# One core, two transformer blocks: the feed-forward's two products of a weight tile in one instruction, and five smaller edits

## The chip, the core and the metric

The kernel runs on one core of a Trainium2 chip. The metric is the device time of one execution in microseconds (us); the kernel before takes 3591.42, the median of three runs (3586.63 to 3591.92). Engines: TensorE (PE, its weight loads PEld), VectorE (DVE), ScalarE (ACT), GpSimd (POOL), SyncE (SP, which issues every DMA here).

## The reference, cut to what matters

256 rows of width 2048, fp32, pass two blocks. Only the widths and the operations around the change stand here.

```python
def first_block(x, c, ...):
    mod = silu(c) @ w_ada + b_ada                       # 2048 x 12288, six parts
    shift1, scale1, gate1, shift2, scale2, gate2 = split(mod, 6)
    p = modulate(rms_norm(x, norm1_w), shift1, scale1) @ w_in   # u 1024, q 512, k 512, v 1024, o 1024, gates 16
    y_f = fourier_mix(u)                                # 2D DFT in 4 groups of 256
    y_m = mlstm_bidirectional(q, k, v, gates) * sigmoid(o)      # 4 heads, normalised rows
    x = x + gate1 * (concat([y_f, y_m]) @ w_out)
    h2 = modulate(rms_norm(x, norm2_w), shift2, scale2)
    a, v = split(depthwise_conv_centred(h2 @ w_up, w_conv, b_conv), 2)   # 2048 x 11264
    x = x + gate2 * ((silu(a) * v) @ w_down)            # 5632 x 2048
    return rms_norm(x, norm_f_w)

def second_block(x, ...):
    h = x + 0.5 * rms(swiglu(rms(x, pre1), w_gate, w_up, w_down), post1)  # 2 x 2048 x 5632, 5632 x 2048
    ...                                  # S5 state space model, sparse attention, gates, out
    return h + 0.5 * rms(swiglu(rms(h, pre2), ...), post2)               # the same widths again
```

## The kernel before

**Number format.** Every large product keeps nearly fp32 accuracy by a split into two parts, hi (`float32r`, ScalarE's copy) and lo (VectorE's difference x - hi). W·x becomes hi·xh + lo·xh + hi·xl, three TensorE products that add up in one PSUM region. Activations lie transposed: 128 features on the partitions, the 256 rows of x along the free axis, so an output tile is 128 x 256 and half of a PSUM bank.

**Weights.** A stream (`STREAMS`) is packed on the host in the order of use, in groups of output tiles; `lin_steps` (L304) goes through the groups, and through a group in chunks of 128 x 1024 weights. `chunk` (L298) loads a chunk of 512 KB by SP into `wr` (4 buffers; in the first mixer every third goes to `wa`, 2 more), ScalarE writes `wh` (3), VectorE `wl` (2). For each k of the chunk the three products run, each over the group's tiles in turn:

```python
for ci, (a, b) in enumerate(((hi, xh), (lo, xh), (hi, xl))):
    for j in js:
        self.mm(outs[j][0:widths[j]], a[:, c:c + widths[j]], b, ...)
```

A group of four tiles takes two banks of the eight. In a stream with `tile_evac` the last group takes a bank for each tile, holds back its last two chunks and ends tile by tile. `matmul` is always called in `mm` (L291), so every matmul has that line; tiles tell them apart.

**Feed-forward.** Three of them: up1/down1 (with convolution), up2/down2, up3/down3. `up` has 44 + 44 output tiles, 22 groups of two a tiles and two v tiles (`_pairs`), 16 k; `down` has 16 output tiles in groups of four, 44 k. `ev_up` (L592, L1157) takes a group's two banks: convolution or scaling, Silu, the product of both halves, and `hidden` (L628) splits it into `hh` and `hl`. `ev_down` (L613, L1171) scales a tile and adds its square; `post_norm` (L1182) then makes the next stage's input, tile by tile, and its split parts. `modulated` (L505) does that ahead of up1.

**Order around it.** `entry` (L638) sums the first two modulation parts (64 chunks of `w_ada1`) on TensorE: `strip_sum` (L470) multiplies by a single column, in four 32-column strips of the array side by side. Between them run the steps of q and k's stream (`next(stream)` twice per outer step). `mix1` (L723) then runs the streams v_in, u_in, o_in, each of 16 chunks; after each chunk `background` steps the generators in `self.bg`: the mLSTM (`mlstm`, L823), the DFT, and `rest` (L555), the modulation parts 2, 4, 3, 1.6 steps a chunk and 1.0 in out1. Part 2 is summed on VectorE (`ada_part`, L446: 32 scaled sums of 128 x 1024), parts 4 and 3 on TensorE (`ada_strips`, L475). `ev_o` forces the rest of the mLSTM at o_in's first group. In `mlstm` a row of a 36 x 256 table is spread over 128 partitions by a matmul with a column of the unit matrix, three times: in `weights` (L889), `values` (L926), and at the end for the norm.

In up2 `s5_tables` (L1001) computes 32 tables (cosine and sine, 128 x 512) in the background and stores them in DRAM; in the second mixer `load_tab` (L1387) loads each and ScalarE appends the negated sine. The order of instructions on each engine is the framework's, from its own schedule, except in two stretches that are written out by hand (`manual_schedule` in `post_norm`).

## Time and profile before

| | |
|---|---|
| runs | 3591.42 us median, 3586.63 to 3591.92 |
| profiled execution | 3595.09 us, span 3593.4 us, mean granted TensorE clock 0.988 |
| TensorE busy | 3508.3 us (98%), 28264 matmuls |
| weight loads busy | 3349.0 us (93%) |
| VectorE busy | 2198.6 us (61%) |
| ScalarE busy | 1594.4 us (44%) |
| POOL busy | 23.8 us (1%) |
| DMA | 710.8 MB, mean 198 GB/s |

"Busy" is the time in which an engine ran at least one instruction; matmuls overlap one another in the records, so the spacing of their starts tells what one costs, not its duration. "Granted clock" is the share of TensorE's 2.4 GHz that it was given (0.5 is its 1.2 GHz level). The streams run in this order (first load issued, us): entry 0, v_in 135, u_in 206, o_in 284, out1 385, up1 489, down1 1014; the second block's feed-forward from about 1280, its mixer from 2054, the last feed-forward from 2801.

### The profile page before, as it was taken

The page shows a single profiled execution, that of the slowest core. Times are in us where ns is not written, and L with a number is a line of the kernel's source. Part 1 is how long each engine was busy: PE and PEld are TensorE (multiplying, and loading weights), DVE is VectorE, ACT ScalarE, POOL GpSimd, SP SyncE. Part 2 cuts the span into 40 slices and gives each one's busy share as a digit, 9 for nine tenths or more (in the row PEclk, how much of TensorE's full clock was granted, in tenths as well). Part 3 has the DMA queues.
Part 4 walks back from the last instruction along what each step waited for, and adds up shares of the span by engine and source line. Part 5 has one row for each costly group of instructions (what it writes and reads, how often), then busy time and mean ns, then how long its engine had stood idle before and what let it go on. Part 6 is the DMA issues. An engine that isn't in the chain of part 4 may idle for free.

```text
span 3593.4 us, 67935 instructions
## 1 busy us (share of the span) xinstructions
PE 3508.3 (98%) x28264; PEld 3349.0 (93%) x28264; DVE 2198.6 (61%) x3146; ACT 1594.4 (44%) x2096; POOL 23.8 (1%) x65
## 2 busy tenths in 40 slices
PE   8999999999999999999999999899999999999997
PEld 4688889999999999999999899789899999999997
DVE  2574467777655479865544589986556655555445
ACT  2343345555444444444433443358744544444333
POOL 0000000000000000000000000000000000000000
PEclk9999999999999999999999999999999999999999
DMA  9886756777555556765555556555455455555554
GB/s 332 308 294 219 271 198 222 230 224 224 182 182 183 184 182 212 225 211 183 182 183 183 173 167 197 160 170 152 139 182 182 153 182 183 183 186 183 182 183 140
DMA packets 213318, 710.83 MB, mean 198 GB/s; under 512 B 23904, under 2 KB 39296, under 8 KB 213008
## 3 DMA queue, kind: packets, MB, share of 16 engines
q1 hardware_dynamic: 213008, 706.48, 61.4%
q8 instruction: 221, 3.62, 0.4%
q14 instruction: 89, 0.73, 0.1%
HBM read 694.29 MB, written 11.57 MB: 196 GB/s over the span
## 4 chain that ended last, share of the span: by engine, by line
PE 92%; DVE 4%; DMA 2%; issue 1%; ACT 1%; SPq 0%; DVEq 0%; ACTq 0%
PE ps L291 92%; DMA wr<-in_w_ada 1%; DVE wl L276 1%; DVE w L276 1%; DVE t L276 1%; DVE r L279 0%; DMA r<-in_xT 0%; PE ps L1637 0%; DVE r L276 0%; DVE w L1416 0%; DMA tab<-d_tab 0%; ACT wh L273 0%; DMA wr<-in_w_qk_in 0%; DMA wa<-in_w_out 0%; DVE rstd L417 0%
## 5 line engine op out<-in xcount | busy, mean ns | idle before, releaser
L276 DVE TENSOR_TENSOR wl<-wr,wh 128x1024 fp32r<-128x1024 f32 x1064 | 1300.6, 1223 | 1106.2 <-PE ps L291 869.1
L273 ACT ACTIVATE wh<-wr 128x1024 fp32r<-128x1024 f32 x1064 | 1126.6, 1059 | 1549.1 <-PE ps L291 1398.3
L291 PE MATMUL ps<-r,wh 128*128 128x256 f32 x12224 | 1762.1, 285 | 26.6 <-ACT r L273 19.1
L291 PEld LDWEIGHTS ps<-r,wh 128*128 128x128 f32 x12224 | 1596.9, 193 | 67.2 <-issue 24.7
L291 PE MATMUL ps<-r,wl 128*128 128x256 f32 x6112 | 1001.6, 286 | 14.9 <-DVE wl L276 14.8
L291 PEld LDWEIGHTS ps<-r,wl 128*128 128x128 f32 x6112 | 850.2, 193 | 35.3 <-DVE wl L276 21.6
L291 PE MATMUL ps<-hh,wl 128*128 128x256 f32 x2112 | 345.0, 283 | 0.0
L291 PE MATMUL ps<-hl,wh 128*128 128x256 f32 x2112 | 345.0, 283 | 0.0
L291 PE MATMUL ps<-hh,wh 128*128 128x256 f32 x2112 | 343.9, 283 | 0.0
L291 PEld LDWEIGHTS ps<-hl,wh 128*128 128x128 f32 x2112 | 294.0, 192 | 0.0
L291 PEld LDWEIGHTS ps<-hh,wl 128*128 128x128 f32 x2112 | 294.0, 192 | 0.0
L291 PEld LDWEIGHTS ps<-hh,wh 128*128 128x128 f32 x2112 | 293.4, 192 | 0.0
L291 PE MATMUL ps<-m,wh 128*128 128x256 f32 x1024 | 154.1, 286 | 0.4 <-ACT wh L273 0.4
L291 PEld LDWEIGHTS ps<-m,wh 128*128 128x128 f32 x1024 | 134.6, 191 | 8.0 <-issue 4.6
L291 PE MATMUL ps<-wr,silu_c 128*32 128x512 f32 x348 | 80.5, 630 | 11.8 <-DMA wr<-in_w_ada 11.7
L279 DVE SCALAR_TENSOR_TENSOR acc<-wr,silu_c,acc 128x1024 f32<-128x1024 f32 x50 | 64.1, 1282 | 35.6 <-DMA wr<-in_w_ada 35.2
L291 PE MATMUL ps<-m,wl 128*128 128x256 f32 x512 | 83.2, 284 | 0.0
L279 DVE SCALAR_TENSOR_TENSOR t<-ps,params,t 128x255 f32<-128x255 f32 x176 | 76.6, 476 | 0.6
L276 DVE TENSOR_TENSOR wl<-wa,wh 128x1024 fp32r<-128x1024 f32 (+1 forms) x34 | 40.8, 1199 | 58.1 <-ACT wh L273 29.1
L291 PEld LDWEIGHTS ps<-m,wl 128*128 128x128 f32 x512 | 70.6, 191 | 3.7 <-DVE wl L276 2.0
L273 ACT ACTIVATE t<-ps 128x256 f32<-128x256 f32 (+2 forms) x87 | 39.3, 458 | 76.0 <-PE ps L291 56.1
L273 ACT ACTIVATE t<-ps,params 128x256 f32<-128x256 f32 x88 | 46.6, 562 | 55.8 <-PE ps L291 34.8
(233 smaller groups left out, 1776.8 us busy)
## 6 DMA issues: line engine op xcount, KB each, us to landing
wr<-in_w_up SPq DMA_DIRECT2D x528, 512.0 KB, 3.7
wr<-in_w_down SPq DMA_DIRECT2D x264, 512.0 KB, 3.6
wr<-in_w_ada SPq DMA_DIRECT2D x141, 512.0 KB, 5.1
wr<-in_w_out SPq DMA_DIRECT2D x53, 512.0 KB, 3.9
wa<-in_w_ada SPq DMA_DIRECT2D x51, 512.0 KB, 5.3
wr<-in_w_ga_in SPq DMA_DIRECT2D x32, 512.0 KB, 3.7
wr<-in_w_glu SPq DMA_DIRECT2D x32, 512.0 KB, 3.7
wr<-in_w_gb_in SPq DMA_DIRECT2D x32, 512.0 KB, 3.6
```

Of the source, the lines that this page charges most:

```text
L273: return self.nc.scalar.activation(out=out, in_=in_, func=func, **kw)
L276: return self.nc.vector.tensor_tensor(out, a, b, op=op)
L279: return self.nc.vector.scalar_tensor_tensor(out=out, in0=a, scalar=s, in1=b, op0=op0, op1=op1)
L291: self.nc.tensor.matmul(out, lhsT, rhs, start=start, stop=stop, skip_group_check=skip)
```

## The change

1. The feed-forward streams run "wide": an activation's xh and xl lie side by side in one 128 x 2 x 256 tile (`pair`, in the ring of now 25 pairs; `hidden` likewise). hi multiplies both at once (512 columns, a whole bank), lo multiplies xh alone into the bank's first half, right behind. An output tile now takes a bank; groups are of two tiles. `fold` adds the two halves of the bank. `ev_up` collects two groups before Silu and product; the post-norm gain moves from `ev_down` to `post_norm`.
2. `v_in` is split; its first half (8 chunks) runs in the entry, one step per outer step, the other half (`vb_in`) in `mix1`. The sums' bank also takes the place of the separate `mods` bank.
3. In `mlstm` the rows go to DRAM (`rows_out`) and come back over 128 partitions (`row_in`), both issued by POOL.
4. While a pool with room is open (`more_lo`), every third low part lies in an extra buffer `wx`.
5. `rest` sums part 2 in strips and parts 4 and 3 on VectorE.
6. The tables are stored with three parts; the negation moves from `load_tab` to `s5_tables`, which runs at 0.34 steps a chunk where it ran at 0.45.

```diff
-    "v_in": ("w_in", 16, _tiles(_cols(O_V, 1024))),
+    "v_in": ("w_in", 16, _tiles(_cols(O_V, 512))),
+    "vb_in": ("w_in", 16, _tiles(_cols(O_V + 512, 512))),
...
-    "up1": ("w_up", 16, _pairs(KF, DFF)),
-    "down1": ("w_down", 44, _tiles(_cols(0, D))),
+    "up1": ("w_up", 16, _singles(KF, DFF)),
+    "down1": ("w_down", 44, _tiles(_cols(0, D), per=2)),
...
+    def fold(self, dst, bank):
+        self.act(dst, bank[:, 1], ACT.Copy)
+        self.tt(dst, bank[:, 0], dst, ALU.add)
+        return dst
...
-        lo = self.new(self.p_w, "wl", [P, CH], F32R, self.NB[2])
+        self.nlo += 1
+        if self.more_lo is not None and self.nlo % 3 == 0:
+            lo = self.new(self.more_lo, "wx", [P, CH], F32R, 1)
+        else:
+            lo = self.new(self.p_w, "wl", [P, CH], F32R, self.NB[2])
...
-            if spread:
+            if wide:
+                outs = banks = [self.ps() for _ in tiles]
+            elif spread:
...
+                        x = act(k)
+                        if wide:
+                            for j in js:
+                                c = (k - k0) * n + starts[j]
+                                self.mm(outs[j], hi[:, c:c + P], x, k == 0, k == kt - 1, True)
+                                self.mm(outs[j][:, 0], lo[:, c:c + P], x[:, 0], False, k == kt - 1, True)
+                            continue
...
             def rest():
-                yield from self.ada_part(2, self.mod[:, 2])
+                yield from self.ada_strips(2, self.mod[:, 2])
                 for part in (4, 3):
-                    yield from self.ada_strips(part, self.mod[:, part])
+                    yield from self.ada_part(part, self.mod[:, part])
...
             def ev_up(gi, banks):
+                if gi % 2 == 0:
+                    self.av = self.t2(), self.t2()
+                for n in range(2):
+                    t = self.fold(self.t1(), banks[n])
+                    conv(self.av[n][:, gi % 2], t, gi + n * KF)
+                if gi % 2 == 1:
+                    a, v = self.av
+                    self.act(a, a, ACT.Silu)
+                    hid.append(self.hidden(ph, a, v))
...
-                self.stt(xs[k], res, self.mod[:, 5, k:k + 1], xs[k], ALU.mult, ALU.add)
+                for part in (1, 0):
+                    self.stt(xs[k], res[:, part], self.mod[:, 5, k:k + 1], xs[k], ALU.mult, ALU.add)
...
                 if qt in (1, 4):
-                    next(stream)
+                    next(streams[0])
+                if qt == 6:
+                    next(streams[1])
...
         def weights(hd, d):
             r = d * 32 + hd
-            mb = self.ps()[:, 0]
-            self.mm(mb, self.eye[0:R, r:r + 1].to_broadcast([R, P]), mrow, True, True)
+            mb = self.row_in(0, r)
...
+    def rows_out(self, n, rows, n_rows=36):
+        self.nc.gpsimd.dma_start(self.d_rows[n, 0:n_rows], rows[0:n_rows])
+
+    def row_in(self, n, r):
+        t = self.t1()
+        d = self.d_rows[n, r]
+        self.nc.gpsimd.dma_start(t, bass.AP(tensor=d.tensor, offset=d.offset, ap=[[0, P], [1, T]]))
+        return t
...
+            self.act(tab[:, 2], tab[:, 1], ACT.Copy, scale=-1.0)
+            nc.sync.dma_start(self.d_tab[j], tab[:, 0:3])
...
-                self.ts(f, res, gp[:, k:k + 1], None, ALU.mult)
-                self.add_square(st, res)
+                f = self.fold(fhalf(), res)
+                self.add_square(st, f)
...
+                self.stt(t, fs[k], gp[:, k:k + 1], r, ALU.mult, ALU.mult)
...
-            nc.sync.dma_start(tab[:, 0:2], self.d_tab[j])
-            self.act(tab[:, 2], tab[:, 1], ACT.Copy, scale=-1.0)
+            nc.sync.dma_start(tab, self.d_tab[j])
```

## Rows read from the trace of the kernel before

**Rows 1.** The page's chain that ended last, shares by engine.

```profile
PE 92%; DVE 4%; DMA 2%; issue 1%; ACT 1%; SPq 0%; DVEq 0%; ACTq 0%
```

**Rows 2.** Stretches: us; busy of PE, PEld, DVE, ACT, POOL; clock; DMA share; GB/s.

```profile
0.00:137.00 137.00, 115.28 (x666) 62.50 (x666) 39.00 (x83) 36.96 (x59) 1.78 (x21) 0.96 0.92 332
137.00:512.00 375.00, 367.03 (x2760) 312.92 (x2760) 201.40 (x260) 145.15 (x231) 5.67 (x16) 0.98 0.74 256
...
2240.00:2410.00 170.00, 152.68 (x1157) 137.47 (x1156) 160.68 (x262) 73.94 (x108) 7.40 (x8) 0.92 0.55 168
...
2800.00:2830.00 30.00, 23.74 (x165) 22.34 (x165) 28.10 (x62) 17.61 (x36) 0.00 (x0) 0.89 0.32 100
2830.00:3300.00 470.00, 470.00 (x3911) 469.74 (x3910) 251.97 (x251) 201.41 (x210) 0.00 (x0) 1.00 0.59 183
```

**Rows 3.** TensorE's timeline in down3: start us, us to the end, what.

```profile
3553.38 0.64 PE L291 MATMUL ps<-hh,wl 128*128 128x256 f32 x4
3553.86 0.64 PE L291 MATMUL ps<-hl,wh 128*128 128x256 f32 x4
```

**Rows 4.** TensorE's timeline at up1's start, granted clock 0.5.

```profile
513.38 1.05 PE L291 MATMUL ps<-r,wl 128*128 128x256 f32 x4
514.23 2.04 PE L291 MATMUL ps<-r,wh 128*128 128x256 f32 x8
```

**Rows 5.** The timeline of gn_in2, whose weights have 48 columns.

```profile
2254.26 0.28 PE L291 MATMUL ps<-r,wl 128*48 128x256 f32 x1
...
2258.69 0.28 PE L291 MATMUL ps<-r,wl 128*48 128x256 f32 x1
```

**Rows 6.** The timeline at down3's end.

```profile
3572.82 0.28 PE L291 MATMUL ps<-hh,wl 128*128 128x256 f32 x1
3572.94 0.28 PE L291 MATMUL ps<-hl,wh 128*128 128x256 f32 x1
...
3573.50 0.59 PE L291 MATMUL ps<-acc,ones_d 128*128 128x256 f32 x2
3573.93 1.46 PE L291 MATMUL ps<-t,ones_d 128*128 128x256 f32 x6
```

**Rows 7.** Groups over the whole span, shapes apart: busy us, mean ns | idle.

```profile
L276 DVE TENSOR_TENSOR wl<-wr,wh 128x1024 fp32r<-128x1024 f32 x1063 | 1299.6, 1223 | 1105.7 <-PE ps L291 869.1 <-issue 103.6 <-ACT wh L273 83.5
...
L279 DVE SCALAR_TENSOR_TENSOR t<-ps,params,t 128x255 f32<-128x255 f32 x176 | 76.6, 476 | 0.6
...
L276 DVE TENSOR_TENSOR t<-hh,hh 128x256 f32<-128x256 f32 x128 | 46.7, 420 | 0.1
...
L273 ACT ACTIVATE t<-ps 128x256 f32<-128x256 f32 x53 | 20.1, 379 | 29.5 <-DVE r L283 15.2 <-PE ps L291 9.8 <-DVE m L283 4.5
...
L276 DVE TENSOR_TENSOR t<-r,rstd 128x256 f32<-128x256 f32 x32 | 12.0, 417 | 0.1
```

**Rows 8.** Groups from 137 to 512 us.

```profile
L279 DVE SCALAR_TENSOR_TENSOR acc<-wr,silu_c,acc 128x1024 f32<-128x1024 f32 x20 | 25.6, 1278 | 2.0 <-DMA wr<-in_w_ada 1.9
...
L291 PE MATMUL ps<-rd,eye 36*128 36x256 f32 x16 | 5.6, 428 | 0.0
L291 PE MATMUL ps<-rm,eye 36*128 36x256 f32 x16 | 5.6, 428 | 0.0
...
L291 PE MATMUL ps<-row,eye 4*128 4x256 f32 x8 | 2.4, 422 | 0.0
```

**Rows 9.** DMA issues: KB each, us to landing.

```profile
w<-d_rel SPq DMA_DIRECT2D x16, 128.0 KB, 4.5
...
d_rel<-t SPq DMA_DIRECT2D x1, 32.0 KB, 4.0
```

**Rows 10.** TensorE's timeline around a set of strip sums in out1.

```profile
393.31 1.05 PE L291 MATMUL ps<-wr,silu_c 128*32 128x512 f32 x4
394.29 0.75 PE L291 MATMUL ps<-m,wl 128*128 128x256 f32 x4
```

**Rows 11.** The negation of a table's sine, whole span.

```profile
L273 ACT ACTIVATE tab<-tab 128x256 f32<-128x256 f32 x32 | 13.3, 415 | 51.3 <-DMA tab<-d_tab 33.3 <-DVE w L276 11.6 <-DVE w L1416 3.9
```

More of the change, by code (lines that the diff above doesn't have):

```diff
@@ L64, in _pairs, with _singles @@
     return out
+def _singles(n_tiles, second):
+    return [[_cols(i * P, P), second + _cols(i * P, P)] for i in range(n_tiles)]
 Q_COLS = np.concatenate([np.concatenate([W2_Q + h * 64 + np.arange(64) for h in pr]) for pr in PAIRS])
@@ L89 @@
     "out2": ("w_out_2", 16, _tiles(_cols(0, D))),
-    "up3": (("ffn2_w_gate_2", "ffn2_w_up_2"), 16, _pairs(KF, DFF)),
-    "down3": ("ffn2_w_down_2", 44, _tiles(_cols(0, D))),
+    "up3": (("ffn2_w_gate_2", "ffn2_w_up_2"), 16, _singles(KF, DFF)),
+    "down3": ("ffn2_w_down_2", 44, _tiles(_cols(0, D), per=2)),
 }
@@ L237, in __init__ @@
         self.more = None
+        self.nlo = 0
+        self.more_lo = None
     def name(self, tag):
@@ L246, in new, with pair, halves, take @@
         return pool.tile(list(shape), dtype, tag=tag, name=self.name(tag), **kw)
-    def ring(self, dtype=F32):
-        return self.new(self.p_ring, "r", [P, T], dtype)
+    def pair(self):
+        return self.new(self.p_ring, "r", [P, 2, T], F32R)
+    def halves(self, pool, tag, bufs=None):
+        left = []
+        def take():
+            if not left:
+                t = self.new(pool, tag, [P, 2, T], F32, bufs)
+                left.extend([t[:, 1], t[:, 0]])
+            return left.pop()
+        return take
     def t1(self, dtype=F32):
@@ L309, in chunk, with lin_steps @@
         return hi, lo
-    def lin_steps(self, stream, act, evac=None, tile_evac=None):
+    def lin_steps(self, stream, act, evac=None, tile_evac=None, wide=False):
         _, kt, groups = STREAMS[stream]
@@ L574, in block1 @@
             self.finish()
-            self.more = None
+            self.more = self.more_lo = None
             del ys
@@ L592, in ev_up @@
             def ev_up(gi, banks):
-                a = self.t2()
-                v = self.t2()
-                for j in range(2):
-                    conv(a[:, j], banks[0][:, j], gi * 2 + j)
-                for j in range(2):
-                    conv(v[:, j], banks[1][:, j], KF + gi * 2 + j)
-                s = self.t2()
-                self.act(s, a, ACT.Silu)
-                hid.append(self.hidden(ph, s, v))
-            self.linear("up1", lambda k: h[k], ev_up)
+                if gi % 2 == 0:
[7 more added lines that the diff above has]
+                    hid.append(self.hidden(ph, a, v))
+            self.linear("up1", lambda k: h[k], ev_up, wide=True)
             self.finish()
@@ L811, in ev_o @@
                 for i in range(2):
-                    hi, lo = self.ring(F32R), self.ring(F32R)
-                    self.split(o[:, i], hi, lo)
-                    yo.append((hi, lo))
+                    x = self.pair()
+                    self.split(o[:, i], x[:, 0], x[:, 1])
+                    yo.append(x)
         self.linear("o_in", act_h, ev_o)
@@ L923, in inverse @@
             nc.vector.reciprocal(rd, dn)
-            held["rd"] = rd
+            self.rows_out(1 + held["pair"], rd)
         def values(hd, d):
@@ L955, in mlstm @@
             a, b = 2 * pair, 2 * pair + 1
+            held["pair"] = pair
             products(a)
@@ L1005, in slot @@
             if not halves:
-                t = self.new(pool, "hh", [P, 2, T])
-                halves.extend([t[:, 0], t[:, 1]])
+                t = self.new(pool, "hh", [P, 4, T])
+                halves.extend(t[:, i] for i in range(4))
             return halves.pop()
@@ L1153, in ffn @@
             hid = []
+            self.more_lo = ph
             if extra is not None:
-                self.bg.append([extra(ph), 0, 0.45])
+                self.bg.append([extra(ph), 0, 0.34])
             def ev_up(gi, banks):
-                g, s, u = self.t2(), self.t2(), self.t2()
-                rb = rstd().unsqueeze(1).to_broadcast([P, 2, T])
-                self.tt(g, banks[0], rb, ALU.mult)
-                self.act(s, g, ACT.Silu)
-                self.tt(u, banks[1], rb, ALU.mult)
-                hid.append(self.hidden(ph, s, u))
-            self.linear(up, lambda k: act[k], ev_up)
+                if gi % 2 == 0:
+                    self.gu = self.t2(), self.t2()
+                for n in range(2):
+                    self.fold(self.gu[n][:, gi % 2], banks[n])
+                if gi % 2 == 1:
+                    g, u = self.gu
+                    rb = rstd().unsqueeze(1).to_broadcast([P, 2, T])
+                    self.tt(g, g, rb, ALU.mult)
+                    self.act(g, g, ACT.Silu)
+                    self.tt(u, u, rb, ALU.mult)
+                    hid.append(self.hidden(ph, g, u))
+            self.linear(up, lambda k: act[k], ev_up, wide=True)
             self.finish()
@@ L1349, in ev_o @@
                     self.tt(b, b, ya[k], ALU.add)
-                    hi, lo = self.ring(F32R), self.ring(F32R)
-                    self.split(b, hi, lo)
-                    mixed.append((hi, lo))
+                    x = self.pair()
+                    self.split(b, x[:, 0], x[:, 1])
+                    mixed.append(x)
             self.linear("o2", lambda k: onsa[k], ev_o)
```

126 lines of the change are left out of this document (68 added, 58 removed).

## The prediction, made before the change was run

> **What bounds the kernel now.** I read the chain of waits first: 92% of it is TensorE at the matmul helper [rows 1]. The table of stretches, read next, says where that holds without exception: in the three feed-forward stretches TensorE is busy 470.0 of 470.0 us and its weight loader 469.7, at full granted clock, while VectorE is busy 251.97 [rows 2]. The other two blocks have the same spacing. A faster VectorE or DMA buys nothing there; fewer or shorter products do. Elsewhere it differs: the first 137 us move 332 GB/s with TensorE busy 115, so DMA bounds them; 137 to 512 us is TensorE's again with 8 us idle; 2240 to 2410 us is VectorE's (160.7 of 170), as is the start of the last feed-forward (28.1 of 30).
>
> The third view is TensorE's timeline in a down stage: four products start at 3553.38 and the next four at 3553.86, so one 128x128 by 256-column product costs 120 ns [rows 3]. One "triple" (hi·xh, lo·xh, hi·xl for one output tile and one k) is 360 ns. Count: up has 88 tiles x 16 k, down 16 x 44, together 2112 triples a feed-forward and 6336 in all: 2281 us of the 3593, spread over three blocks.
>
> **The change part by part. 1: wide products.** hi·xh and hi·xl become one 512-column product into a whole bank, lo·xh stays at 256 columns: two weight loads instead of three, the same 768 columns. So the gain is whatever of the 120 ns is not streaming. Where the granted clock is 0.5 (the 1.2 GHz level) four products of the same kind take 0.85 us, 213 ns each, which is 256 columns at one per cycle and nothing on top [rows 4]; at 2.4 GHz the columns alone would be half of it, 106.7, so 13.3 ns of the 120 are something else. Two rows say what. With 48 weight columns instead of 128 the spacing falls: 39 products between 2254.26 and 2258.69, 113.6 each [rows 5]. So some 6.5 ns hang on the weight load and 6.8 on the product itself. And a plain fp32 product with 128x128 weights holds the array 0.43 us for two, 215 ns, with its load entirely hidden [rows 6]. No row has a 512-column product of this type, so its cost is bounded: 213.3 + 2 = 215 by the fp32 row, which is as long; 213.3 + 6.8 = 220 if the product's own part stays and the load hides behind the longer stream; 226.7 if all 13.3 stay; 240 at worst, if the extra time grows with the columns. I take 220, since it alone uses rows of this very product type and needs only that 213 ns hide a load which 120 nearly hide. The triple is then 220 + 120 = 340, and 20 ns x 6336 = **127 us** gained (ends: 360 - 335 = 25 ns, 158 us; and nothing).
>
> The Trainium skill (TensorE: Matmul & The Clock Gate, Back-to-back issue gap) gives the gap of a single product as columns over 2.4 GHz plus a fixed 2.5 ns. That would be 109.2 for 256 columns, which the measured 120 refutes here; by it alone the triple would go from 327.5 to 325 and the gain, 2.5 ns x 6336, would be 16 us.
>
> That lo·xh follows hi at once into the same bank costs nothing by the trace: the last held products of the last down stage run one tile at a time, so back to back into one half bank, and still start 0.12 us apart (3572.82, 3572.94) [rows 6].
>
> The price of it: every tile needs a fold, 0.38 us on ScalarE and 0.42 on VectorE [rows 7], and groups of two tiles end twice as often. A chunk of 1024 weight columns lasts 8 triples, 2.72 us. VectorE needs in up1 per chunk 1.22 for the low part, 0.48 for the convolution (four of 0.48 a group of four chunks), 0.17 for the hidden split, a quarter of 1.28 for the modulation sums [rows 7, 8], and the folds' 0.21: 2.4 of 2.72. In up2 the tables take 0.34 steps of six products (0.42 each [rows 7], an estimated 0.35 apart) a chunk, 0.7, and the total is about 2.5. Tight, but under. The third low-part buffer lets it run 2 chunks (5.4 us) ahead, so I put the steady stretches at nothing; if that cover fails, the rival below prices it.
>
> Starts get worse, for TensorE now eats the first group in 16 x 0.68 = 10.9 us where it took 23, while its inputs come no faster. In up3 VectorE makes an input with two products and one scaled sum (0.42, 0.42, 0.48 [rows 7], an estimated 1.1 us together as ends overlap) and a low part of 1.22 per four: 22 us, 11 us of waiting where some 6 were lost before (23.7 busy of 30 [rows 2]): **+5**. In up1 two scaled sums a k make an estimated 17, 6 us of waiting against some 3 lost to the half clock there [rows 4]: **+4**. Up2's inputs come out of the down stage tile by tile, now two at the end instead of four: 0. Post-norm takes the gain along (0.48 in place of 0.42, 16 times [rows 7]) and the last tile is folded before its square (0.8): **+2** at mix2's start, **+2** at the end.
>
> **2: entry and first mixer.** Half of v is 8 chunks x 24 products x 0.12 = 23 us of TensorE, taken out of the stretch it bounds. In the entry its 4.2 MB cost 12.6 us at 332 GB/s, and say 1.4 for its last products: **-23 + 14**. The entry's idle time on TensorE holds the 23 us. Row broadcasts: three groups of matmuls, 5.6 + 5.6 + 2.4 us busy, of which I count 12 because ends overlap [rows 8]: **-12**. In their place POOL issues 4 writes and 20 reads. The before trace has no POOL transfer; the nearest are SP's small d_rel ones, 4.0 out and 4.5 us back [rows 9]. Read first by ScalarE's Relu and by VectorE's scaling: behind those two wait conversions of weights, and behind these TensorE, with two chunks in hand (5.8 us). The rows of a pair leave two steps before they are read, so 8.5 us of transfers meet some three chunks of 2.88, 8.6. I take 0; if all 24 stood bare it would be some 100 us, but none is issued right at its use. On POOL itself only the triangular selects queue behind them. Which modulation part is strip-summed: TensorE's set of strips costs 0.98 us until the next product [rows 10], 16 sets a part and an estimated tenth more for switching between product types, so one part less is **-17**; VectorE gets 32 x 1.28 = 41 us more in 137 to 512, where it is busy 201 of 375 [rows 2, 8]: about 233 of 320 after, still under. The steps come out at 64 + 32 of 99, so three are left at the end of out1, where two 1.28 us sums stand before up1's gain: **+3**. Sum of this part: -35.
>
> **3: tables in DRAM.** The negation (32 x 0.415 us on ScalarE, each behind a tab load [rows 11]) leaves the VectorE-bound stretch; ScalarE's conversions no longer stand behind it. Ends 0 and 13 us; I take **-3**. Stored in up2, ScalarE has room.
>
> Sum: -127 + 13 - 35 - 3 = **-152 us**. The profiled execution took 3595.1 (span 3593.4), 3.7 above the median of 3591.4, so I forecast 3443 for such a run and 3440 as the median.
>
> **The rivals.** (a) All 13.3 ns stay with every product: triple 346.7, gain 84, total 3482. For it: the weight load might disturb any stream alike; against it, the fp32 row. (b) The extra time goes with the columns: 6.5 to 0 ns a triple, 41 to 0 us, leaving 3525 to 3566. For it: 4-byte columns at full clock never show less than 113.5 here. Against: none shows at half clock. If only the fixed part that the fp32 row shows is saved, 215 - 213 = 2 ns a triple, the gain is 13 us and the time 3554; the chance of that alone I put at 0.03, since 13.3 ns are there to be had. The rule of the Trainium skill named above is of this kind. (c) The first mixer gains nothing, because the broadcasts' round trips hold up ScalarE and VectorE: +35, 3475. (d) Slower: a group's end stalls TensorE, because folds wait for the bank at the head of ScalarE's and VectorE's queues and the next chunks' conversions stand behind them. There are 3 x (44 + 8) = 156 ends; the bare price is copy 0.38 + add 0.42 + low part 1.22 = 2.0 us, 312 us in all, total 3750. It turns the sign from 152 / 156, about 1 us an end. Against it: today's ends, with longer evacuations, show no idle time, and TensorE has its chunks in hand. (e) The change doesn't reach the array, if a 512-column product were run as two of 256: it is (b)'s worst end.
>
> **How the numbers follow.** Forecast (triple 335 to 342) 0.54, (a) 0.22, (b) with (e) 0.16, (c) alone 0.03, (d) 0.03, anything else 0.02. The forecast's own range is 3405 to 3460; to leave out no more than 2 in 10 the range reaches over (a) and half of (b): 3400 to 3525. Faster by over 0.2% (7 us, about what a measurement here can tell from no change) 0.95, within 0.01, slower 0.04.
>
> **What would show it.** Right: matmuls of 128x512 about 220 ns before their successor, those of 256 with the low part 120, feed-forward stretches of some 718 us, the weight loader no longer busy all the time. Entry near 150 us, up1 starting near 477 us. Wrong: 227 or 240 in that spacing, idle time of TensorE released by the fold or by wl at group ends, or ScalarE waiting for row transfers in the first mixer.

## The result, and the profile after

The changed kernel takes 3542.09 us (median of four runs, 3536.85 to 3545.96) against 3589.75 for the kernel before (3586.63 to 3591.92): a ratio of 0.9867, with a 95% interval of 0.985 to 0.9884. The profiled execution has a span of 3535.1 us where it was 3593.4. The change is a gain of 48 us by the medians, 58 by the two profiles; 152 were forecast, and the time lies above the range of 3400 to 3525.

The page of the kernel after, busy time and chain (the chain answers to [rows 1]):

```profile
PE 3419.5 (97%) x21760; PEld 2988.0 (85%) x21760; DVE 2342.3 (66%) x3458; ACT 1662.0 (47%) x2381; POOL 40.5 (1%) x89
...
PE 61%; DVE 3%; ACT 0%; issue 0%; DMA 0%; SPq 0%; DVEq 0%; ACTq 0%
```

28264 matmuls have become 21760, and the weight loader is no longer busy all the time: that much is as described. TensorE still bounds the kernel (the named shares of this chain add up to two thirds only, so its 61% against 92% is not read as a loss).

The stretches, with the columns of [rows 2], where the feed-forward and the two ends of the second mixer answer to it:

```profile
0.00:137.00 137.00, 117.34 (x735) 70.49 (x736) 42.54 (x85) 39.60 (x60) 1.78 (x21) 0.98 0.89 325
137.00:474.00 337.00, 322.78 (x2524) 290.32 (x2523) 235.43 (x296) 141.72 (x224) 17.70 (x40) 0.99 0.85 297
...
2748.00:2778.00 30.00, 18.81 (x74) 14.47 (x73) 27.28 (x63) 16.32 (x36) 0.00 (x0) 0.77 0.28 87
2778.00:3248.00 470.00, 470.00 (x2686) 409.40 (x2685) 292.59 (x340) 227.47 (x300) 0.00 (x0) 1.00 0.59 187
```

In 470 us of up3 and down3 TensorE is still busy 470.0, at full granted clock. Nothing keeps it waiting there; its products are simply longer than forecast. Its timeline in down3 says how long (answers to [rows 3]; `wl` and `wx` are both low parts):

```profile
3510.24 0.40 PE L317 MATMUL ps<-hh,wh 128*128 128x512 f32 x1
3510.47 0.28 PE L317 MATMUL ps<-hh,wl 128*128 128x256 f32 x1
3510.59 0.40 PE L317 MATMUL ps<-hh,wh 128*128 128x512 f32 x1
3510.83 0.28 PE L317 MATMUL ps<-hh,wl 128*128 128x256 f32 x1
3510.95 0.40 PE L317 MATMUL ps<-hh,wh 128*128 128x512 f32 x1
```

From start to start a 512-column product takes 0.23 to 0.24 us and the low one behind it 0.12. Over the 1256 products of either kind between 2800 and 3240 us the means are 234.0 and 115.9 ns, in down3 235.9 and 116.7. A triple is therefore 350 ns in an up stage and 352 in a down stage, not 340.

At the half clock (answers to [rows 4]) the same two products stand 0.42 and 0.22 us apart, so there the columns alone set the time, 213 ns per 256, as before:

```profile
475.17 0.63 PE L317 MATMUL ps<-r,wh 128*128 128x512 f32 x1
475.59 0.41 PE L317 MATMUL ps<-r,wl 128*128 128x256 f32 x1
475.81 0.63 PE L317 MATMUL ps<-r,wh 128*128 128x512 f32 x1
```

Where the time went by stage, from the starts of TensorE's products in the two traces (up1 and up3 begin with their first product, a down stage with the first product of the hidden part; up2 runs from down1's last product, "second mixer" from down2's last product to up3's first):

| | up1 starts | up1 | down1 | up2 | down2 | second mixer | up3 | down3 | tail |
|---|---|---|---|---|---|---|---|---|---|
| before | 512.4 | 514.7 | 253.3 | 517.4 | 253.3 | 753.3 | 515.2 | 253.3 | 20.4 |
| after | 474.4 | 521.1 | 252.4 | 497.2 | 250.7 | 759.8 | 506.9 | 251.2 | 21.4 |

The three up stages have the same number of products. Up2 gained 20 us, up3 8, and up1 lost 6; the down stages gained 1 to 3. The first mixer gained 38, the second lost 6.5.

Up1's waits show what is different there. The view of waits from 474 to 995 us (waiter, what it waited for, us in total, times, longest us):

```profile
DVE acc L299 <- DMA wr<-in_w_ada: 84.1, 29, 4.6
...
PE ps L317 <- DVE wl L296: 10.7, 14, 1.5
PE ps L317 <- DVE r L299: 7.3, 1, 7.3
PE ps L317 <- DVE wx L296: 5.4, 7, 1.2
```

and the same view of the kernel before, from 512 to 1028 us:

```profile
DVE acc L279 <- DMA wr<-in_w_ada: 33.3, 28, 3.3
...
PE ps L291 <- DVE wl L276: 1.3, 2, 1.0
```

VectorE waits 84 us for the weights of the last modulation part (33 before), and TensorE waits 16 us for low parts (1.3 before). One such place on VectorE's timeline, then on SyncE's and on TensorE's:

```profile
733.92 1.22 DVE L296 TENSOR_TENSOR wl<-wr,wh 128x1024 fp32r<-128x1024 f32 x1
739.77 1.28 DVE L299 SCALAR_TENSOR_TENSOR acc<-wr,silu_c,acc 128x1024 f32<-128x1024 f32 x1 [4.63 <-DMA wr<-in_w_ada]
740.98 0.42 DVE L296 TENSOR_TENSOR t<-ps,t 128x256 f32<-128x256 f32 x1
741.31 1.22 DVE L296 TENSOR_TENSOR wl<-wr,wh 128x1024 fp32r<-128x1024 f32 x1
```

```profile
734.03 0.33 SPq L496 DMA_DIRECT2D wr<-in_w_ada  x1
```

```profile
740.55 0.64 PE L317 MATMUL ps<-r,wh 128*128 128x512 f32 x2
742.58 0.50 PE L317 MATMUL ps<-r,wl 128*128 128x256 f32 x2 [1.39 <-DVE wl L296]
```

The load is issued at 734.03, when the raw buffer that `wx`'s conversion read (732.78 to 734.00) comes free: SyncE's wait before this load, 1.6 us, ends with that conversion. VectorE has nothing before the sum in its order, so it stands 4.63 us until the data is there; behind the sum stand a fold and the low part that TensorE needs next. TensorE runs through the chunks in hand and idles 1.39 us. Between 490 and 990 us this happens at 22 places behind a 512-column product, about every second group of the 44: 24.2 us lie between starts there where 22 x 0.234 = 5.1 is the rule, **19 us** lost.

One more wait is new, once in each down stage, where the held-back chunks are finished tile by tile. In down1 (995 to 1250 us) it is TensorE's only one; the kernel before shows none in that stage:

```profile
PE ps L317 <- ACT t L293: 1.8, 1, 1.8
```

A last tile's square needs its fold first (in down1, its two scaled adds), and the sum of squares (`ps<-t,ones_d`) stands in TensorE's order ahead of the next tile's products.

### The profile page after: what moved, and what is told of

Same layout as the page of the kernel before. It is cut to its first block, busy times and chain, and to the rows that moved or that the text cites. A ratio compares the mean times of both kernels' runs of the same rounds, so it can differ in the third digit from the quotient of the medians.

```text
span 3535.1 us, 54991 instructions
## 1 busy us (share of the span) xinstructions
PE 3419.5 (97%) x21760; PEld 2988.0 (85%) x21760; DVE 2342.3 (66%) x3458; ACT 1662.0 (47%) x2381; POOL 40.5 (1%) x89
## 4 chain that ended last, share of the span: by engine, by line
PE 61%; DVE 3%; ACT 0%; issue 0%; DMA 0%; SPq 0%; DVEq 0%; ACTq 0%
PE ps L317 61%; DVE w L296 1%; DVE wl L296 1%; DVE t L296 0%; DVE t L299 0%; DVE r L296 0%; PE ps L1712 0%; DVE w L1491 0%; DVE r L299 0%; ACT wh L293 0%; ACT t L293 0%; DVE rstd L458 0%; DVE t L1268 0%; DMA w<-m 0%; ACT r L293 0%
## 5 line engine op out<-in xcount | busy, mean ns | idle before, releaser
L317 PE MATMUL ps<-r,wh 128*128 128x512 f32 (+2 forms) x8000 | 2033.5, 346 | 29.6 <-DVE r L299 15.3
L317 PEld LDWEIGHTS ps<-r,wh 128*128 128x128 f32 (+1 forms) x8000 | 1278.5, 190 | 234.4 <-issue 21.6
L296 DVE TENSOR_TENSOR wl<-wr,wh 128x1024 fp32r<-128x1024 f32 x786 | 959.6, 1221 | 607.2 <-ACT wh L293 464.3
L317 PE MATMUL ps<-r,wl 128*128 128x256 f32 (+2 forms) x4496 | 1044.9, 283 | 16.4 <-DVE wl L296 16.4
L317 PEld LDWEIGHTS ps<-r,wl 128*128 128x128 f32 (+2 forms) x4496 | 765.6, 191 | 47.9 <-DVE wl L296 25.5
L317 PE MATMUL ps<-hh,wh 128*128 128x512 f32 x2112 | 742.7, 398 | 0.0
L296 DVE TENSOR_TENSOR wx<-wr,wh 128x1024 fp32r<-128x1024 f32 x279 | 341.1, 1223 | 237.4 <-ACT wh L293 237.0
L317 PE MATMUL ps<-r,wx 128*128 128x256 f32 x1616 | 418.2, 282 | 8.5 <-DVE wx L296 8.5
L317 PEld LDWEIGHTS ps<-r,wx 128*128 128x128 f32 x1616 | 294.8, 190 | 23.1 <-DVE wx L296 12.2
L317 PE MATMUL ps<-hh,wx 128*128 128x256 f32 x704 | 195.8, 280 | 0.0
L299 DVE SCALAR_TENSOR_TENSOR t<-t,params,t 128x255 f32<-128x255 f32 x176 | 84.1, 480 | 3.0
```

The source lines that it names most:

```text
L296: return self.nc.vector.tensor_tensor(out, a, b, op=op)
L299: return self.nc.vector.scalar_tensor_tensor(out=out, in0=a, scalar=s, in1=b, op0=op0, op1=op1)
L317: self.nc.tensor.matmul(out, lhsT, rhs, start=start, stop=stop, skip_group_check=skip)
```

## The experiments

All twelve kernels start from the changed one. Each was timed beside the kernel before, whose median was 3590.85 us beside e1 to e4, 3588.83 beside e5 to e8 and 3589.76 beside e9 to e12; ratios are to these. The stage times of the table above, for the runs that the text uses:

| | up1 starts | up1 | up2 | second mixer | span | median, ratio |
|---|---|---|---|---|---|---|
| after | 474.4 | 521.1 | 497.2 | 759.8 | 3535.1 | 3542.09, 0.9867 |
| e1: wide product as two | 476.7 | 524.8 | 512.2 | 748.3 | 3576.3 | 3582.36, 0.9975 |
| e2: part 5 in strips | 479.4 | 521.3 | 497.2 | 748.5 | 3528.4 | 3531.03, 0.9835 |
| e3: no third low buffer in up1 | 487.3 | 508.2 | 497.4 | 750.6 | 3530.6 | 3532.16, 0.9841 |
| e4: e3, own buffer for the sums | 485.1 | 502.0 | 497.5 | 751.0 | 3521.8 | 3524.62, 0.9814 |
| e5: a 48-column stream wide | 483.4 | 514.2 | 497.2 | 753.5 | 3530.2 | 3531.93, one run |
| e6: low products behind both high | 484.0 | 496.5 | 495.8 | 749.7 | 3505.8 | 3504.93, 0.9764 |
| e7: tables in two parts | 482.1 | 517.2 | 497.2 | 761.2 | 3541.8 | 3542.53, 0.9866 |
| e8: rows by matmul | 495.4 | 513.6 | 497.2 | 752.5 | 3544.0 | 3540.06, 0.9857 |
| e9: e6 and e3 | 483.1 | 517.1 | 495.3 | 750.0 | 3529.1 | 3533.94, 0.9844 |
| e10: e6 and e4 | 475.6 | 506.4 | 495.3 | 752.9 | 3518.3 | 3519.84, 0.9799 |
| e11: v's half not in the entry | 481.6 | 521.3 | 497.2 | 751.6 | 3535.6 | 3537.28, 0.9855 |
| e12: strips as before | 520.5 | 519.3 | 497.2 | 746.2 | 3566.4 | 3568.81, 0.9943 |

Three cautions come with it. Ten of these profiles (after, e1 to e7, e9, e10) leave the code up to up1 alone, and in all of them the instructions of each engine stand in the same order up to 462 us (strip sums that start together aside). Up1 still starts anywhere from 474.4 to 487.3 us, on average at 481. In e3, 6 us of its 13 arose before the mixer's first load (issued at 155.0 us for 148.7), with the entry's loads running slower (compare 325 GB/s above):

```profile
0.00:137.00 137.00, 115.84 (x692) 70.37 (x694) 40.66 (x78) 36.91 (x56) 1.78 (x21) 0.94 0.85 311
```

So one profile tells a start of up1 to within some 6 us only. Up1 itself varies too: in the six profiles that share its code (after, e5, e7, e8, e11, e12) it takes 513.6 to 521.3 us, 517.8 on average, and e5's 514.2 comes with the instructions in the order of after on every engine up to 2197 us. Nor are the stages beyond it fixed: the second mixer, whose code the kernel after shares with e1 to e4, e6 and e8 to e12, takes 746 to 760 us, because the framework puts its instructions in another order when something far away changes. Where VectorE's sequence there is the same, the times are close: 759.8 and 761.2 in after and e7, 750.6 and 749.7 in e3 and e6. A total that moves by less than some 12 us is therefore read by its stage.

### What the width of a product does

**e1**, the high product split in two, everything else wide:

```diff
-  self.mm(outs[j], hi[:, c:c + P], x, k == 0, k == kt - 1, True)
+  self.mm(outs[j][:, 0], hi[:, c:c + P], x[:, 0], k == 0, k == kt - 1, True)
+  self.mm(outs[j][:, 1], hi[:, c:c + P], x[:, 1], False, k == kt - 1, True)
```

> One part undone, on the changed kernel: hi by xh and xl is issued as two 256-column products into the two halves of the bank; tiles, groups, folds and order stay. Theory A (a column of this type costs some 0.44 ns at full clock, however many stand in a product; merging saves only what a third weight load added): the spacing is 117 to 120 ns for each of the three, 354 to 360 ns a triple where the changed kernel has 350.5, so 3542 + 22 to 60 = 3565 to 3600 us. Rival (merging itself saves nothing, the gain of 48 us is all from the mixers): triple 350 again, 3542 within 5.

Measured: 3582.36 us (0.9963 to 0.9987 of before). Its timeline in down3:

```profile
3539.91 0.40 PE L317 MATMUL ps<-hh,wh 128*128 128x256 f32 x2
3540.16 0.28 PE L317 MATMUL ps<-hh,wl 128*128 128x256 f32 x1
3540.28 0.40 PE L317 MATMUL ps<-hh,wh 128*128 128x256 f32 x2
```

Three products in 0.37 to 0.36 us; over the whole trace 120 ns each. The six feed-forward stages sum to 2329.9 us here, against 2279.5 after and 2307.2 before. So the wide instruction itself is worth 50 us in these stages, and the form around it (folds, groups of two, faster starts) costs 23.

**e5**, `gn_in2`, whose weights have 48 columns [rows 5], made wide too:

```diff
-  self.linear("gn_in2", act_u, ev_gn)
+  self.linear("gn_in2", act_u, ev_gn, wide=True)
```

(its evacuation folds the bank first).

> On the changed kernel: the small stream gn_in2, whose weight tiles have 48 columns, also runs wide, so the trace holds 16 products of 512 columns whose weight load is short, each followed by one of 256. Theory A (the extra time goes with the columns): 2 x 113.6 = 227 ns for the 512 columns. Rival C (each product carries a fixed part of 6.8 ns, and the 234 of the changed kernel is a 220 plus what a load of 128 columns disturbs): 220. The 256-column ones 113 to 114 in both. The time stays within 5 us of 3542.

Measured, TensorE's timeline there:

```profile
2199.65 0.28 PE L317 MATMUL ps<-r,wl 128*48 128x256 f32 x1
2199.77 0.39 PE L317 MATMUL ps<-r,wh 128*48 128x512 f32 x1
2200.00 0.28 PE L317 MATMUL ps<-r,wl 128*48 128x256 f32 x1
2200.12 0.39 PE L317 MATMUL ps<-r,wh 128*48 128x512 f32 x1
```

0.23 us after a 512-column product, 0.12 after a 256-column one. Leaving out the first of the sixteen pairs, whose 512 columns take 276 ns, the means are 230 and 116 ns. With a weight load of 48 columns the 512-column product still doesn't come near 220. It costs twice the 256-column one: the time above one column per cycle belongs to the columns. The time, 3531.93 in a single run, is 10 us below the 3542 that was expected within 5; the starts and stages above vary by as much.

**e6**, the same products in another order, for each k first the high products of both tiles, then the low ones:

```diff
   for j in js:
       c = (k - k0) * n + starts[j]
       self.mm(outs[j], hi[:, c:c + P], x, k == 0, k == kt - 1, True)
+  for j in js:
+      c = (k - k0) * n + starts[j]
       self.mm(outs[j][:, 0], lo[:, c:c + P], x[:, 0], False, k == kt - 1, True)
```

> On the changed kernel: for a k, both tiles' 512-column products first, then both tiles' 256-column ones, in place of tile by tile. Theory A (a column costs what it costs, and a load of 128 columns hides as soon as a stream is longer than it): the 512-column products stay at 232 to 236 ns; the 256-column ones are 120 where the next load goes behind a 256-column stream, as in the kernel before, and 117 or less otherwise: triple 350 to 354, total 3540 to 3565. Rival (lo straight behind hi in the same bank costs something): triple under 348, total under 3530.

Measured: 3504.93 us (0.975 to 0.9779), the fastest of all. The total is the one that the rival expected (under 3530), but the triple is neither's. The spacing changes by little: 233.1 and 115.4 ns between 500 and 975 us, a triple of 348.5 ns and so some 1.5 less than in up3 of the kernel after, whether a 512-column product follows another one into another bank or a low one:

```profile
3000.47 0.39 PE L317 MATMUL ps<-r,wl 128*128 128x256 f32 x2
3000.70 0.63 PE L317 MATMUL ps<-r,wh 128*128 128x512 f32 x2
```

What changed is up1, 496.5 us where it was 521.1 (513.6 at the least in the six profiles that share after's up1). Another 10 us of the total lie in the second mixer, 749.7 for 759.8, which e6's edit leaves alone. Up1's waits from 484 to 980 us:

```profile
DVE acc L299 <- DMA wr<-in_w_ada: 47.0, 29, 3.6
...
PE ps L317 <- DVE r L299: 7.0, 1, 7.0
```

TensorE waits for no low part any more. VectorE's timeline shows a likely reason:

```profile
734.16 1.28 DVE L299 SCALAR_TENSOR_TENSOR acc<-wr,silu_c,acc 128x1024 f32<-128x1024 f32 x1 [1.50 <-DMA wr<-in_w_ada]
735.36 1.22 DVE L296 TENSOR_TENSOR wl<-wr,wh 128x1024 fp32r<-128x1024 f32 x1
736.50 0.75 DVE L296 TENSOR_TENSOR t<-ps,t 128x256 f32<-128x256 f32 x2
```

The framework now puts the low part right behind the sum and both folds after it, and VectorE's wait is 1.5 us instead of 4.6.

### What stalls up1

**e2**, the last modulation part summed in strips on TensorE; no sum is left on VectorE:

```diff
-  self.bg = [[self.ada_part(5, self.mod[:, 5]), 0, 0.25]]
+  self.bg = [[self.ada_strips(5, self.mod[:, 5]), 0, 0.25]]
```

> On the changed kernel: modulation part 5, summed in the background of up1, goes to TensorE's strips in place of VectorE. Theory A (up1 loses some 22 us because VectorE stands in front of sums whose weights have not landed, 84 us in all, and the folds and low parts behind them are late): TensorE's waits for low parts in up1 go from about 22 us to under 4, the strips cost about 18, total 3535 to 3542. Rival B (the folds fill VectorE, whatever the sums wait for): the waits stay at 15 us or more, total 3550 to 3560.

Measured: TensorE waits for no low part in up1 (its only wait is the 6.0 us at the start), yet up1 takes 521.3 us, because the strips are TensorE's own work. The stall goes with the sums on VectorE; moving them to TensorE costs what the stall did. (The total, 3531.03, is below the 3535 to 3542 expected, for the second mixer took 748.5 us.)

**e3**, no third low-part buffer in up1:

```diff
-            self.more_lo = ph
```

> On the changed kernel: no third low-part buffer in up1 and down1 (the other two feed-forwards keep it). Theory A: VectorE runs less far ahead, reaches the modulation sums later after their load was issued and waits less there (84 us towards the 35 of before), but has less in hand: TensorE's waits in up1 anything from 10 to 30 us, total 3530 to 3550. Rival B (VectorE is simply full): less cover only hurts, waits over 30 us, total over 3550.

Measured: up1 508.2, 13 us shorter than in the profile of after and 5 to 13 shorter than in the six profiles that share after's up1. From 487 to 996 us:

```profile
DVE acc L299 <- DMA wr<-in_w_ada: 36.3, 30, 2.3
...
PE ps L317 <- DVE wl L296: 6.4, 12, 1.2
```

The buffer that was to let VectorE run ahead lets it run ahead into the wait for the sum's data: 84.1 us of that wait with it (78.0 to 84.1 in the six), 36.3 without.

**e4**, e3 with one raw buffer kept for these loads (in the room of the third low buffer, so that the two could not be had together):

```diff
-  raw = self.raw()
+  raw = self.raw() if pool is None else self.new(pool, "wy", [P, CH], F32, 1)
...
-  self.bg = [[self.ada_part(5, self.mod[:, 5]), 0, 0.25]]
-  self.more_lo = ph
+  self.bg = [[self.ada_part(5, self.mod[:, 5], ph), 0, 0.25]]
```

> As the run without the third low-part buffer in up1, but the modulation loads get a buffer of their own, so each load is issued as soon as the sum before it is done, some 11 us ahead. Theory A: VectorE no longer waits for these loads (under 5 us), TensorE's waits in up1 go under 5 us, total 3515 to 3527. Rival B: VectorE's wait goes but TensorE's stays above 15 us, total as the run without the third buffer.

Measured: up1 502.0. From 485 to 988 us:

```profile
DVE acc L299 <- DMA wy<-in_w_ada: 17.1, 20, 2.1
...
PE ps L317 <- DVE wl L296: 1.7, 5, 0.7
```

The load no longer waits for a low part's conversion to free its buffer, and TensorE's wait for low parts, 16.1 us in the kernel after and 6.4 in e3, falls to 1.7. VectorE's own wait, expected under 5 us, is still 17.1. Up1's 502.0 stands 4.5 above up2's 497.5.

**e9** (e6's order without the third buffer) and **e10** (e6's order with e4's buffer):

> Low products behind both tiles' high ones, and no third low-part buffer in up1. If the later use of the low part is what freed up1 (each low part is needed one 512-column product later), up1 stays near 497 us with little waiting of TensorE for low parts (under 4 us), and the total is within 6 us of the 3505 that the reordering gave with the third buffer. If it was the order on VectorE that happened to come with the third buffer (low part ahead of the two folds behind a modulation sum), up1 goes back to 507 to 515 us with 10 to 20 us of waits, and the total is 3515 to 3525.

> The reordering, no third low-part buffer, and the modulation loads of up1 in a buffer of their own. Both together as a best version: the own buffer alone took up1 from 521 to 502, the reordering alone to 496.5 with VectorE still waiting 47 us for these loads. If those waits are covered now, nothing is left to gain: up1 495 to 498, total 3503 to 3508. If they still cost TensorE something, up1 falls under 494 and the total under 3503.

Measured: e9's up1 takes 517.1, with 15.2 us of waiting for low parts; e10's 506.4, with 6.0. So the reordering does not free up1 by itself: with it the third buffer is worth 21 us, without it the same buffer costs 5 to 13. E9's stage was expected at 507 to 515 and came out worse (and the total at 3533.94, 9 above its expectation); e10's was expected at 495 to 498, with a total of 3503 to 3508, and both came out 8 to 12 us above. VectorE waits about as long for the sums' loads in e9 (49.1 us) as in e6 (47.0), so the length of that wait alone does not set what TensorE loses. That fits e6's gain being one of order on VectorE, as its timeline shows; but product order and VectorE's order changed together in all these kernels, and no kernel with the one alone was run. Why the third buffer turns from harm to help stays open to that extent. The two remedies don't add up either: e10 is 15 us slower than e6.

### The first mixer, and the tables

**e11**, v's first half out of the entry again:

```diff
-                if qt == 6:
-                    next(streams[1])
...
+        self.linear("v_in", act_h, self.ev_v(vfm))
         self.linear("vb_in", act_h, self.ev_v(vfm))
```

> The first half of v moved out of the entry and back to the mixer, nothing else. The working of the prediction (23 us less in the mixer, 14 us more in the entry) says that up1 starts about 9 us later than the 474 after the change: 483, total +9. If the entry carried the half for less than 14 us, up1 starts later than that, up to 23 us: 497. If its end waits ate the gain, up1 starts at 474 or before.

Measured: up1 starts at 481.6, the mean of the ten profiles with that half in the entry. The mixer's first load is issued at 128 us instead of 148 to 156, and the mixer takes 353 us instead of 324 to 335: what the one gains the other gives. The move is worth nothing that these profiles show.

**e8**, rows spread over the partitions by matmul again, three places of this kind:

```diff
-            mb = self.row_in(0, r)
+            mb = self.ps()[:, 0]
+            self.mm(mb, self.eye[0:R, r:r + 1].to_broadcast([R, P]), mrow, True, True)
```

> On the changed kernel: the mLSTM's rows are spread by matmuls again, nothing goes through DRAM. The prediction counts 12 us of TensorE for them in a stretch that TensorE bounds: total 3550 to 3556, the stretch from the entry's end to out1's end 12 longer. Rival (c): the round trips hold up ScalarE and VectorE by as much as they save: 3542 within 4.

Measured: up1 starts at 495.4, 14 us after that mean (8 after the latest of the ten), and the mixer takes 340.5 us from its first load, where the ten take 324 to 335. The total, 3540.06, is what rival (c) expected: up1 and the second mixer came out 7 us shorter each, and neither is far from what the same code takes in other profiles. By the stage, in one profile, the rows are worth 12 to 14 us. For the kernel after, the transfers read as follows (KB each, us to landing), and the waits on them from 137 to 474 us:

```profile
t<-d_rows POOLq DMA_DIRECT2D x20, 128.0 KB, 7.5
...
d_rows<-rd POOLq DMA_DIRECT2D x2, 36.0 KB, 4.1
```

```profile
ACT pt L293 <- DMA t<-d_rows: 6.0, 4, 2.3
DVE vh L299 <- DMA t<-d_rows: 4.1, 1, 4.1
```

ScalarE waits 6 us for rows, and TensorE for none of it.

**e12**, part 2 on VectorE and parts 4 and 3 in strips, as before the change:

```diff
-                yield from self.ada_strips(2, self.mod[:, 2])
+                yield from self.ada_part(2, self.mod[:, 2])
                 for part in (4, 3):
-                    yield from self.ada_part(part, self.mod[:, part])
+                    yield from self.ada_strips(part, self.mod[:, part])
```

> Modulation part 2 summed on VectorE and parts 4 and 3 in strips again, as before the change, nothing else. The prediction's price is 17 us of TensorE for one part more in strips, less 3 for the sums in front of up1: up1 starts near 488, total +14. If the strips lie in TensorE's idle time, or VectorE bounds the first mixer, the start stays within 4 us of 474.

Measured: up1 starts at 520.5, 39 us after the mean, and the median is 3568.81. The groups of strip sums (busy us, mean ns), first in e12 from 137 to 520 us, then in the kernel after from 137 to 474:

```profile
L317 PE MATMUL ps<-wr,silu_c 128*32 128x512 f32 x190 | 42.4, 613 | 0.0
...
L317 PE MATMUL ps<-wa,silu_c 128*32 128x512 f32 x100 | 28.0, 621 | 2.9 <-DMA wa<-in_w_ada 2.9
```

```profile
L317 PE MATMUL ps<-wr,silu_c 128*32 128x512 f32 x108 | 21.1, 604 | 0.0
...
L317 PE MATMUL ps<-wa,silu_c 128*32 128x512 f32 x40 | 10.5, 604 | 0.0
```

TensorE is busy with strips 70.4 us against 31.6. Of the 142 products more, 128 are the additional part and 14 belong to the entry's sums, which end later here. Over all its work up to up1's start TensorE is busy 477 us, where the ten profiles have 440 to 449: most of the 39 us is its own work, the rest waiting.

**e7**, tables stored in two parts and the sine negated after the load:

```diff
-            nc.sync.dma_start(tab, self.d_tab[j])
+            nc.sync.dma_start(tab[:, 0:2], self.d_tab[j])
+            self.act(tab[:, 2], tab[:, 1], ACT.Copy, scale=-1.0)
```

> On the changed kernel: tables of two parts again, with the negation on ScalarE in the second mixer. The second mixer takes 759.8 us in the changed kernel and 753.2 in the kernel before. If the three-part tables did that (larger loads, or what they do to the order): 753 within 2, total 3535. If not (post-norm, or the order that the framework chose for other reasons): 759 to 763, total 3540 to 3550.

Measured: 3542.53, second mixer 761.2 against 759.8. VectorE's sequence there is the same in both. The negation was neither a burden there nor is its removal the reason why that mixer is longer after the change.

## Why the prediction was wrong

**The step that failed: "I take 220".** The prediction split the 120 ns of a product into 106.7 of streaming and 13.3 fixed, called 6.5 of these the weight load's and 6.8 the product's, and let a 512-column product pay the 6.8 once. The runs show an extra that grows with the columns: 234.0 - 213.3 = 20.7 ns on 512 and 115.9 - 106.7 = 9.2 on 256. The evidence that misled was [rows 6]: fp32 products of 128x256 at 215 ns, nearly 213.3 and with the load hidden; that is another type of product, as the prediction said, and it does not carry over. [Rows 4] carried the other half of it: at half clock nothing stands on top of the columns, neither a fixed extra nor a proportional one, so that row could not tell them apart, and it was read as if it spoke for the fixed one. Why a column at full clock takes more than one cycle of it stays open.

What the wide form saves hangs on the weight loads, as e5 confirms from the other side: 48 columns of weights instead of 128 shorten the 256-column product from 120 to 113.6 where every product has its own [rows 5], but hardly change the wide triple, 346 for 350. The prediction took this for 6.5 ns on every product. Two facts fit a pace better. In the kernel before, the loads start 120 ns apart, as the products do, and the loader is busy 469.7 of 470 us [rows 2]:

```profile
2999.83 0.55 PEld L291 LDWEIGHTS ps<-r,wh 128*128 128x128 f32 x4
3000.31 0.55 PEld L291 LDWEIGHTS ps<-r,wl 128*128 128x128 f32 x4
```

And in e6, where half of the products are long, a low product right behind another, each with a 128-column load of its own, takes 114.6 ns (means from 2800 to 3220 us). So 120 looks like the pace of loads that follow one another, and some 115 like what 256 columns cost by themselves; no run was made to separate the two. With 10 ns saved on 1408 triples and 8 on 704, a feed-forward gains 19.7 us, all three **59** instead of 127. That is 68 of the 94 us by which the profiled span's gain of 58 misses the 152.

It is rival (b), the extra that goes with the columns, whose price was 353.5 to 360 a triple, 3525 to 3566 in all, at a chance of 0.16. The median of 3542 lies inside. Its triple was too dear by 3 ns, because a low product behind a long one takes 116 and not 120; that its total came out right is luck, owed to the losses in up1 and the down stages, which it did not hold. Rival (a) is refuted by the triple (346.7 would have been 226.7 and 120). So is (e) at its price of 360 a triple; whether the engine runs 512 columns as two of 256 inside, these rows don't tell.

The Trainium skill (TensorE: Matmul & The Clock Gate, Back-to-back issue gap) gives the gap of a single product as columns over 2.4 GHz plus 2.5 ns: 215.8 for 512 columns and 109.2 for 256. This type of product takes 234 and 116 here; the extra is not 2.5 ns once, but doubles with the columns. The gain by that rule would have been 16 us; the columns gave 59.

**"I put the steady stretches at nothing"** failed in up1. By its products it should have become 14.1 us shorter; it became 6.4 longer, so **20.5 us** were lost, 19 of them at the 22 places (13 to 21 in the six profiles with up1's code). Rival (d) named the place, a group's end with folds and conversions in one queue, but not the mechanism, and its price of up to 2.0 us at every end does not show: folds take 0.38 and 0.42 us as forecast, and with as many of them up3 is busy 470.0 of 470 us and up2 comes within 4.4 us of its products (1408 x 0.35). Nor is VectorE full: it is busier in up2, 402.6 of 497.0 us, than in up1, 385.1 of 521.1, and TensorE waits 0.6 us in all there. What holds VectorE is a load of modulation weights, issued only when a raw buffer comes free, with the sum next in line and a fold and a low part behind it. The third buffer made that wait longer (e3), a buffer of its own removes most of it (e4), and without the sums TensorE waits for no low part (e2). How a stall passes from VectorE to TensorE hangs on the order of instructions as well (e6, e9), and that share was not separated. The prediction counted the sums' 1.28 us in VectorE's budget and not the wait in front of them, though the trace of before has it (33.3 us).

**The down stages** were given their products' gain whole, 5.6 us each, and got 0.9, 2.6 and 2.1: **11 us** less in all. Some 5 of these are the new wait of 1.6 to 1.8 us before each end. The prediction looked at the folds of the last tile, not at the square behind each fold. The other 6 were not traced.

**Starts.** Up3: 11 us of waiting were forecast where some 6 were lost; 30 - 18.81 = 11.2 measured, against 30 - 23.74 = 6.3 [rows 2]: right, +5. (The granted clock of the same windows is 0.77 for 0.89, which the prediction did not count.) Up1: a gap of 7.3 us where it was 3.9, +3.4 for +4: the size was right, but it came as one wait ahead of up1's first product, in the mixer's column, and not inside its first group. Up2, put at 0, gained 20.2 where its products give 14.1: -6. The end: +1 for +2.

**Entry and first mixer, -35.** The two profiles give 512.4 - 474.4 = 38, the mean of ten 31: the sum was right, and two of its three terms were not. V's move was put at -9 and is worth nothing (the entry pays 20 to 28 us for it, not 14). The rows were put at -12 and are worth 12 to 14 (e8): right. The strips were put at -17 and are worth 39 when they alone are undone: the prediction counted 16 sets a part where there are 32, and no run shows the tenth that it added for switching. A row that was not read would have said so. In the kernel before, from 137 to 512 us, two parts are 256 strip products, 128 or 32 sets of four each:

```profile
L291 PE MATMUL ps<-wr,silu_c 128*32 128x512 f32 x176 | 35.9, 604 | 0.0
...
L291 PE MATMUL ps<-wa,silu_c 128*32 128x512 f32 x80 | 21.0, 604 | 0.0
```

32 x 0.98 is 31 us. Undone one by one the three come to 53 us, while together they gave 31 to 38, so they overlap; what takes the place of the gain, when all are there, was not separated. Rival (c), waits on the rows' round trips, did not come: none of TensorE's waits is on them.

**Tables, -3:** nothing (e7). **Second mixer, +2:** +6.5, of which the order of its instructions can be all, as 746 to 760 us in kernels with the same code there show.

The sum by the two profiles: -59 (columns) + 20.5 (up1) + 11 (down stages) - 6 (up2) + 6 (up3, its start with it) - 38 (entry and first mixer) + 6.5 (second mixer) + 1 (end) = -58. Against the forecast of -152 it is the first three terms, 68, 20.5 and 11, that were missed; the others differ by little and cancel.

**The best version measured** is e6, 3504.93 us: the change with the low products behind both high ones, 37 us faster than the change as it was made and 2.4% faster than the kernel before.

## What to carry to other kernels

Whether the time above one column per cycle is fixed or goes with the columns decides what a wider instruction is worth; another type of product doesn't tell, so where no row shows it the two cases deserve like chances, and a kernel with one small stream made wide (e5), or with the wide product split again (e1), settles it. An extra buffer for one producer lets its engine run ahead only as far as the next wait in that engine's order; look first for a load whose buffer is freed by that very engine. When the same instructions in the same order take 7 us more or less in one stage (up1), a single profile settles no smaller difference there. A count of instructions belongs to the page's own count for their group, not to a reading of the code.

## What the runs showed of the hardware

- `float32r` products at full granted clock run at about 2.2 columns per ns, 512 in 234 ns and 256 in 116, back to back with hidden weight loads, and this hardly depends on the weights' width (230 and 116 with 48 columns) or on which bank comes next (233.1 and 115.4 in e6). At half clock the same products take 213 ns per 256 columns, with nothing on top. Where every product has 256 columns and its own 128-column load, it takes 120, and the loads start 120 ns apart too.
- The entry, with the same instructions in the same order, ran its loads at 310 to 326 GB/s in ten executions; up1's start moved by up to 13 us in these.
- A read of one row of 256 values to 128 partitions, issued by POOL, lands after 7.5 us (median of 20), a write of 36 rows after 4.1, while the core's DMA moved 297 GB/s; the nearest transfers of SyncE in the trace of before took 4.5 and 4.0 [rows 9].
